# Two layers of a streaming encoder: a second buffer for a convolution's replicated input, the copies into it issued before the previous convolution, and one statistics pass for v

## The chip, the cores and the metric

The kernel runs on the 8 cores of one Trainium2 chip. Every core takes two prompt sequences of 2048 tokens and one sample group of 64 tokens; the cores do not talk to each other. The metric is the device time of the slowest core in microseconds (us), lower is better. Some executions, of the kernel before and of most of the others, were in a slower state: one die or both were granted a lower TensorE clock (in the slowest, of 5269 us, cores 0 to 3 had 0.806 to 0.808 and the others 0.972 to 0.974).

## The reference

Two layers, each with one projection of 13312 columns that feeds three branches, a gated merge and an output projection:

```python
h = rmsnorm(x, norm_g)
a_b, a_c, a_x, a_z, b_in, b_z, c_u, c_v, c_z, g_a, g_b, g_c = split(h @ w_in)
# A: short gated convolution of 3 taps
y_a = a_b * dwconv3(a_c * a_x) * silu(a_z)
# B: Conformer convolution module, 31 taps for each channel
glu = b_in[..., :W_B] * sigmoid(b_in[..., W_B:])
y_b = silu(layernorm(dwconv31(glu) + bias)) * silu(b_z)
# C: spatial gating over chunks of 128 tokens
v   = layernorm(gelu(c_v))
y_c = gelu(c_u) * (W_s @ v + b_s) * silu(c_z)
m = sum_k sigmoid(g_k + gate_b_k) * (y_k @ w_branch_k)
x = x + m @ w_out          # after two layers: a last rmsnorm
```

## The kernel before

A core cuts its tokens into nine tiles: five of 512 columns, three of 384 and, with the sample group, one of 448. I call one tile through one layer a *pass*; there are 18, in the order layer 0 of two tiles, layer 1 of the same two, then the next two tiles. Passes 1 to 9 and 11 have 512 columns, 10 and 12 to 16 have 384, the last two 448.

A helper records each operation with what it reads and writes, and derives the semaphores. So all ScalarE work has one line (L241), all TT work another (L244), and one reads by tile names. Four places matter.

**Branch B.** The 31-tap convolution is done by TensorE as 8 x 4 small matmuls with banded weights (`dB_t`, the taps). It needs the gated input four times, shifted by one column each (`grep`, made from `gluT` by 16 small copies that SyncE issues). A pair is two groups of 128 channels:

```python
grep = sb("grep", (128, 2, GB, PW), BF16)            # one buffer, one pair
def replicate(q):                                    # 16 copies, SyncE's queue
    for s4 in range(4):
        for g in range(GB):
            dma_start(out=grep[32*s4:32*s4+32, :, g, 0:wb],
                      in_=gluT[32*g:32*g+32, qb, :, s4:s4+wb])
def conv_b(j):                                       # reads grep and dB_t of j
    ...
    if j + 3 < 8: load_dB(j + 3)                     # taps, SyncE's queue, 3 buffers

stage_B1(0); replicate(0); stage_A(0)
for q in range(1, 4):
    stage_B1(q)
    conv_b(2*q-2); conv_b(2*q-1)
    replicate(q)                                     # after the convolutions that read grep
    stage_A(2*q-1); stage_A(2*q)
conv_b(6); conv_b(7); stage_A(7)
```

**v.** Gelu of a chunk of 128 tokens goes to `gv_t`, two buffers; after every second chunk `cv_stats` makes mean and 1/deviation (Sqrt on ScalarE, reciprocal on VectorE) and normalises two chunks.

**Weights.** They come as fp32 through GpSimd's queue (`wring<-w`, cast to bf16 on the way) until a block has been stored to memory as bf16 (`c<-wring`, SyncE's queue); from then on it is read as bf16 (`wring<-c`). Which visit of a block stores it is fixed by `(2, 0, 3, 1, 2, 1)[order % 6]`. A ring of four slots holds the blocks in use. A store is issued when its block is first used.

**Branch C and the merge.** co is normalised a stage at a time among branch C's stages; in the merge, m0+m1 is added after the third product.

## Time and profile before

| | before |
|---|---|
| median of 4 runs, one of them (4820.46) slow | 4750.1 us (4725.02 to 4820.46) |
| TensorE busy, profiled core | 4306.4 of 4726.6 us |
| granted clock, eight cores | 0.968 to 0.972 |

From the page of the kernel before: the span, TensorE's line of busy times, the digits of its busy share, of the granted clock and of the DMA engines in 40 slices, and the chain of work that ended last.

```profile
span 4726.6 us, 74121 instructions; the slowest of 8 cores (4691.4 to 4726.6 us)
PE 4306.4 (91%) x25860; PEld 2117.0 (45%) x25860; DVE 2024.8 (43%) x3476; ACT 1708.8 (36%) x2816; POOL 214.1 (5%) x607
PE   6897978979999999989999999989898999999897
PEclk8998999989999999999999999999999999999999
DMA  8898987988887658776574555474655555665453
PE 65%; DMA 10%; SPq 7%; DVE 7%; issue 6%; ACT 4%; DVEq 0%; POOL 0%; ACTq 0%; POOLq 0%
```

TensorE (PE) is the bottleneck, the DMA engines are nearly full in the first quarter only, and 17% of the chain is DMAs and their issuing.

The view of waits, TensorE alone, of the kernel before: who waited for whom, us in total, number of waits, longest.

```profile
PE ps L715 <- DMA grep<-gluT: 223.0, 32, 21.4
PE ps L507 <- ACT tmp_t L241: 46.5, 55, 2.6
PE ps L507 <- DVE tmp_t L247: 19.9, 43, 1.2
PE ps L897 <- DVE vm L244: 18.5, 18, 2.3
PE ps L557 <- DVE hT L244: 17.7, 6, 7.9
```

L715 is the convolution, L507 every projection, L897 the output projection. Over half of TensorE's 420 idle us is the convolution waiting for the copies.

One such wait in the timeline of TensorE, pass 6 of the kernel before (start, length, what, count, and in brackets the idle time before it and who ended it):

```profile
1534.75 16.57 PE L507 MATMUL ps<-hT,wring 128*128 128x512 bf16 x76
1561.73 6.07 PE L715 MATMUL ps<-grep,dB_t 128*32 128x512 bf16 x64 [10.41 <-DMA grep<-gluT]
```

TensorE stands still for 10.41 us, and then the 64 small matmuls take 6.07 us. Without a wait, 32 of them take 1.9 us. The record of the granted clock in the trace shows why: it stands at half from 1556.5 to 1566.7 us and at full afterwards.

The view of stretches of the kernel before, for passes 2 and 9 (512 columns) and 13 (384): window, its length, busy us of each engine with counts, granted clock, DMA share, GB/s.

```profile
336.00:627.00 291.00, 263.04 (x1430) 118.55 (x1428) 119.20 (x188) 100.26 (x172) 20.66 (x38) 0.96 0.91 188
2350.00:2615.00 265.00, 258.76 (x1422) 117.42 (x1420) 119.59 (x183) 98.18 (x150) 8.10 (x31) 1.00 0.54 175
3314.00:3533.00 219.00, 199.87 (x1379) 114.52 (x1378) 96.44 (x179) 84.33 (x146) 7.46 (x30) 0.98 0.61 203
```

Pass 9 shows what a 512-column pass costs when hardly anything waits: 258.76 us of work at clock 1.00. Pass 2 takes 26 us more, at 91% DMA.

### The profile page before, as it was taken

The numbers are of one execution on the slowest core, as the hardware profiler recorded it, in microseconds if no ns is written. First come the engines' busy times: TensorE is split into PE (matmuls) and PEld (weight loads), VectorE is DVE, ScalarE is ACT, GpSimd is POOL, SyncE is SP. The second block draws the span as 40 slices with busy tenths as digits, with TensorE's granted clock in tenths as the row PEclk, the third lists the DMA queues.
The fourth block names the chain that finished last, engine by engine and source line by source line (L and its number), as shares of the span: only waits on it lengthen the run. The fifth ranks groups of instructions, "written<-read, shape, count | busy, mean of one in ns | idle before, by whom it ended". The sixth has DMA issues, their size and how long they took to land.

```text
span 4726.6 us, 74121 instructions; the slowest of 8 cores (4691.4 to 4726.6 us)
## 1 busy us (share of the span) xinstructions
PE 4306.4 (91%) x25860; PEld 2117.0 (45%) x25860; DVE 2024.8 (43%) x3476; ACT 1708.8 (36%) x2816; POOL 214.1 (5%) x607
## 2 busy tenths in 40 slices
PE   6897978979999999989999999989898999999897
PEld 2343433434444444444444454445454555544444
DVE  2533534335353343535344353534344443545353
ACT  3332423334333342433343343334333433433332
POOL 1000000000000000000000000000000000000000
PEclk8998999989999999999999999999999999999999
DMA  8898987988887658776574555474655555665453
GB/s 174 159 175 194 186 166 156 176 208 187 206 204 193 190 167 197 176 203 198 169 221 143 193 184 181 146 225 171 217 184 191 192 189 193 212 200 178 150 175 127
DMA packets 234715, 869.22 MB, mean 184 GB/s; under 512 B 34512, under 2 KB 108848, under 8 KB 178032
## 3 DMA queue, kind: packets, MB, share of 16 engines
q1 hardware_dynamic: 195840, 648.75, 41.9%
q0 software_dynamic: 37952, 214.84, 25.0%
q8 instruction: 216, 3.54, 0.3%
q14 instruction: 147, 1.20, 0.1%
q10 hardware_dynamic: 560, 0.88, 0.1%
HBM read 874.87 MB, written 93.85 MB: 205 GB/s over the span
## 4 chain that ended last, share of the span: by engine, by line
PE 65%; DMA 10%; SPq 7%; DVE 7%; issue 6%; ACT 4%; DVEq 0%; POOL 0%; ACTq 0%; POOLq 0%
PE ps L507 50%; SPq L682 7%; PE ps L715 6%; DMA grep<-gluT 4%; PE ps L897 4%; PE ps L557 3%; DVE tmp_t L247 3%; DMA c<-wring 2%; DMA wring<-w 1%; ACT cs_t L241 1%; ACT L241 1%; ACT gv_t L241 1%; DVE co L244 1%; DVE yc L244 1%; PE ps L700 1%
## 5 line engine op out<-in xcount | busy, mean ns | idle before, releaser
L507 PE MATMUL ps<-hT,wring 128*128 128x512 bf16 (+2 forms) x13824 | 2770.7, 359 | 93.6 <-ACT tmp_t L241 46.5
L507 PEld LDWEIGHTS ps<-hT,wring 128*128 128x128 bf16 x13824 | 1343.3, 98 | 1438.0 <-issue 131.3
L241 ACT ACTIVATE tmp_t<-ps 128x512 f32<-128x512 f32 (+2 forms) x882 | 473.9, 556 | 938.6 <-PE ps L507 798.4
L247 DVE SCALAR_TENSOR_TENSOR tmp_t<-tmp_t,ps 128x512 f32<-128x512 f32 (+2 forms) x576 | 365.4, 634 | 827.3 <-PE ps L507 577.3
L241 ACT ACTIVATE tmp_t<-ps,pc 128x512 f32<-128x512 f32 (+2 forms) x432 | 274.9, 645 | 729.8 <-PE ps L507 729.5
L715 PE MATMUL ps<-grep,dB_t 128*32 128x512 bf16 (+2 forms) x5120 | 301.9, 390 | 239.0 <-DMA grep<-gluT 223.0
L244 DVE TENSOR_TENSOR tT<-ps,tmp_t 128x512 bf16<-128x512 f32 (+2 forms) x160 | 94.7, 592 | 843.5 <-PE ps L507 667.0
L241 ACT ACT_TABLE_LOAD x179 | 229.7, 1283 | 302.4 <-DVE tmp_t L247 95.6
L715 PEld LDWEIGHTS ps<-grep,dB_t 128*32 128x32 bf16 x5120 | 138.9, 107 | 399.0 <-issue 332.8
L241 ACT ACTIVATE co<-ps,pc 128x512 f32<-128x512 f32 (+2 forms) x144 | 93.1, 646 | 505.6 <-PE ps L715 505.4
L557 PE MATMUL ps<-wring,hT 128*128 128x512 bf16 (+1 forms) x1056 | 240.5, 389 | 23.0 <-DVE hT L244 17.7
L897 PE MATMUL ps<-wring,vm 128*128 128x512 bf16 (+1 forms) x1056 | 232.9, 381 | 20.6 <-DVE vm L244 18.5
L507 PE MATMUL ps<-yc,wring 128*128 128x512 bf16 (+2 forms) x1152 | 248.3, 358 | 0.0
L507 PE MATMUL ps<-yb,wring 128*128 128x512 bf16 (+2 forms) x1152 | 248.3, 358 | 0.0
L507 PE MATMUL ps<-ya,wring 128*128 128x512 bf16 (+2 forms) x1152 | 248.3, 358 | 0.0
L247 DVE SCALAR_TENSOR_TENSOR tmp_t<-tT,pc,tmp_t 128x512 f32<-128x512 bf16 (+2 forms) x320 | 208.5, 652 | 36.3 <-DVE tmp_t L247 1.6
L267 POOL DMA_DIRECT2D wring<-w x188 | 103.0, 548 | 1827.4 <-PE ps L507 1015.3
L557 PEld LDWEIGHTS ps<-wring,hT 128*128 128x128 bf16 (+1 forms) x1056 | 104.9, 100 | 153.3 <-issue 35.9
L241 ACT ACTIVATE cs_t<-ps,pc 128x512 bf16<-128x512 f32 (+2 forms) x288 | 169.4, 644 | 0.0
L897 PEld LDWEIGHTS ps<-wring,vm 128*128 128x128 bf16 (+1 forms) x1056 | 102.5, 98 | 145.8 <-issue 27.6
L241 ACT ACTIVATE xn_t<-X 128x1024 bf16<-128x1024 f32 (+1 forms) x99 | 103.7, 1050 | 176.0 <-DVE X L247 168.6
L507 PEld LDWEIGHTS ps<-yc,wring 128*128 128x128 bf16 x1152 | 112.7, 98 | 112.0
(101 smaller groups left out, 2525.2 us busy)
## 6 DMA issues: line engine op xcount, KB each, us to landing
wring<-c SPq DMA_DIRECT2D x284, 1024.0 KB, 6.2
wring<-c SPq DMA_DIRECT2D x212, 768.0 KB, 4.4
wring<-w POOLq DMA_DIRECT2D x112, 1024.0 KB, 11.7
wring<-w POOLq DMA_DIRECT2D x76, 768.0 KB, 9.4
c<-wring SPq DMA_DIRECT2D x44, 1024.0 KB, 10.6
grep<-gluT SPq DMA_DIRECT2D x640, 67.6 KB, 3.9
dB_t<-dball SPq DMA_DIRECT2D x128, 256.0 KB, 7.5
c<-wring SPq DMA_DIRECT2D x32, 768.0 KB, 9.1
```

The source lines that it names most:

```text
L241: S.op("act", lambda e: e.activation(out=out, in_=in_, func=func, **kw), reads=reads, writes=writes)
L244: S.op(eng, lambda e: e.tensor_tensor(out=out, in0=in0, in1=in1, op=op), reads=reads, writes=writes)
L247: S.op("dve", lambda e: e.scalar_tensor_tensor(out=out, in0=in0, scalar=scalar, in1=in1, op0=op0, op1=op1), reads=reads, writes=writes)
L267: S.op(eng, lambda e: e.dma_start(out=out, in_=in_), reads=reads, writes=writes, lane=lane)
L507: ins = e.matmul(bank_ap(b, NT), lhsT=w[:, kk, col0:col0 + 128], rhs=rhs[:, kk, 0:NT], start=(kk == 0), stop=(kk == 7))
L557: ins = e.matmul(ps[0:rows, (b2 + h) * 512:(b2 + h + 1) * 512], lhsT=hT[:, kk, c0:c0 + rows], rhs=wV[h][0][:, kk, :], start=(kk == 0), sto ...
L682: return e.dma_start(out=grep[32 * s4:32 * s4 + 32, :, g, 0:wb], in_=gluT[32 * g:32 * g + 32, qb, :, s4:s4 + wb])
L700: e.matmul(bank_ap(bS1, NT), lhsT=ones[:, :], rhs=cs_t[:, 2 * ci, 0:NT], start=(j == 0), stop=(j == 7))
L715: ins = e.matmul(ps[32 * g:32 * g + 32, b * 512 + c0:b * 512 + c0 + n], lhsT=dB_t[:, d, (g * MB + m) * 32:(g * MB + m + 1) * 32], rhs=grep ...
L897: ins = e.matmul(ps[0:rows, (b2 + h) * 512:(b2 + h + 1) * 512], lhsT=mT[:, kk, c0:c0 + rows], rhs=wO[h][0][:, kk, :], start=(kk == 0), sto ...
```

## The change

Its intent is to let the copies of a pair start before the previous convolution has ended and to put more work between them and the convolution. The space for the second buffer comes from `gv_t` and `cbq`. Several small edits come along. The diff, cut to its core:

```diff
-        grep = sb("grep", (128, 2, GB, PW), BF16)
+        grep = sb("grep", (128, 2, 2, GB, PW), BF16)
-        gv_t = sb("gv_t", (128, 2, D), F32)
-        cbq = sb("cbq", (128, DEPTH, NCH * GB * MB), F32)
+        cbq = fg[:, 0:DEPTH * NCH * GB * MB].rearrange("p (l n) -> p l n", l=DEPTH)
 # copies and convolution use grep[:, qb]; the order of the stages:
-  B1(0) rep(0) A(0) | B1(1) conv(0,1) rep(1) A(1) A(2) | B1(2) conv(2,3) rep(2) A(3) A(4)
-  | B1(3) conv(4,5) rep(3) A(5) A(6) | conv(6,7) A(7)
+  B1(0) rep(0) A(0) | B1(1) rep(1) A(1) conv(0,1) | B1(2) rep(2) A(2) conv(2,3)
+  | B1(3) rep(3) A(3) A(4) conv(4,5) A(5) conv(6,7) A(6) A(7)
 # v: gelu of chunk s goes to scratch tiles 2s, 2s+1; statistics once, after the last chunk
-            ACT(c(12), c(8), AF.Sqrt, ...); RECIP(c(16), c(12), ...)
+            ACT(c(12), c(8), AF.Ln, ...);   ACT(c(16), c(12), AF.Exp, ..., scale=-0.5)
-                if s % 2 == 1 or s == NS - 1:
-                    cv_stats(done, s + 1)
+            cv_stats()                       # after the loop; the same Ln, Exp in norm_rs
 # bf16 stores of weights, one block earlier (AHEAD = 1)
-            if n in to_store:
-                DMA(wloc(l, key, True)[0], wring[:, s, 0:8 * w], ...)
+            for i in range(n, n + AHEAD + 1):
+                if i in to_store: ...
 # branch C: co normalised every second stage, the last two in the z stages
-                if j < 6: co_norm(j + 2)
+                if j % 2 == 1: co_norm(2 + j // 2)
 # merge: m0 + m1 before the third product is there
+                    if i == 2: TT(m0, m0, m1, ALU.add, ...)
```

Left out: some preparations of the first two passes (a mask multiplication on VectorE in place of a GpSimd operation; two loads moved from GpSimd's queue to ScalarE's).

More of the change, by code (lines that the diff above doesn't have):

```diff
@@ L19 @@
 NTMP = 9
+AHEAD = 1
 GB = 4
@@ L227, in build_program @@
         ones = sb("ones", (128, 128), BF16)
+        tri = sb("tri", (128, 128), F32)
         epsc = sb("epsc", (128, 1), F32)
@@ L256, in TS @@
                                                     op1=op1), reads=reads, writes=writes)
-        def RECIP(out, in_, reads, writes):
-            S.op("dve", lambda e: e.reciprocal(out=out, in_=in_), reads=reads, writes=writes)
         def COPY(out, in_, reads, writes, eng="dve"):
@@ L321, in build_program @@
             plan += [(l, ("CV", 0)), (l, ("CV", 1))]
-            plan += [(l, ("B1", 0)), (l, ("A", 0))]
-            for q in range(1, 4):
-                plan += [(l, ("B1", q)), (l, ("A", 2 * q - 1)), (l, ("A", 2 * q))]
-            plan += [(l, ("A", 7))]
+            for q in range(4):
+                plan += [(l, ("B1", q)), (l, ("A", q))]
+            plan += [(l, ("A", j)) for j in range(4, 8)]
             plan += [(l, ("CUZ", q)) for q in range(4)]
@@ L375, in wget @@
             w = 384 if key[0] in B384 else 512
-            if n in to_store:
-                DMA(wloc(l, key, True)[0], wring[:, s, 0:8 * w], (("w", s),), (("wall", l, key),), "ws%d" % s)
+            for i in range(n, n + AHEAD + 1):
+                if i in to_store:
+                    to_store.discard(i)
+                    dst_bf, wi = wloc(plan[i][0], plan[i][1], True)
+                    si = i % NSLOT
+                    DMA(dst_bf, wring[:, si, 0:wi], (("w", si),), (("wall",) + plan[i],), "ws%d" % si)
             return wring[:, s, 0:8 * w].rearrange("p (k n) -> p k n", k=8), (("w", s),)
@@ L407, in build_program @@
         S.op("pool", lambda e: e.memset(ones[:], 1.0), writes=("ones",))
+        S.op("pool", lambda e: e.memset(tri[:], 1.0), writes=("tri",))
+        S.op("pool", lambda e: e.affine_select(out=tri[:], in_=tri[:], pattern=[[1, 128]], compare_op=ALU.is_ge, fill=0.0,
+                                               base=0, channel_multiplier=-1), reads=("tri",), writes=("tri",))
         S.op("pool", lambda e: e.memset(rid[:], 0.0), writes=("rid",))
@@ L415, in build_program @@
         ring_pump(2)
-        DMA(cbq[:, :, :], cvb_in.rearrange("l p n -> p l n"), (("X", 0, 1),), ("cbq",), "p1", eng="act")
+        DMA(cbq[:, :, :], cvb_in.rearrange("l p n -> p l n"), (("X", 0, 1),), ("fg",), "p1", eng="act")
         for l in range(DEPTH):
@@ L428, in prep_late @@
             DMA(chal_b[:, :, :, :].rearrange("p a b c -> p (a b c)"), cb_in, (), ("chal_b",), "p5", eng="pool")
-            DMA(fg[:, :], final_g.partition_broadcast(128), (), ("fg",), "p6", eng="act")
         def prep_loads(l):
-            DMA(ybf[:, 0:D], w_sq[l], (), ryb, "p2", eng="pool")
-            DMA(ycf[:, 0:D], b_s[l].partition_broadcast(128), (), ryc, "p2", eng="pool")
+            DMA(ybf[:, 0:D], w_sq[l], (), ryb, "p2", eng="act")
+            DMA(ycf[:, 0:D], b_s[l].partition_broadcast(128), (), ryc, "p3", eng="act")
         def prep_ws(l):
             wl = ybf[:, 0:D]
-            S.op("pool", lambda e: e.affine_select(
-                out=wl.rearrange("p (g q) -> p g q", g=8), in_=wl.rearrange("p (g q) -> p g q", g=8),
-                pattern=[[0, 8], [1, 128]], compare_op=ALU.is_ge, fill=0.0, base=0, channel_multiplier=-1),
-                reads=ryb, writes=ryb)
-            COPY(wsT[:, l].rearrange("p g q -> p (g q)"), wl, ryb, (("wsT", l),))
+            TT(wsT[:, l], wl.rearrange("p (g q) -> p g q", g=8), tri[:, :].unsqueeze(1).to_broadcast([128, 8, 128]), ALU.mult,
+               ryb + ("tri",), (("wsT", l),))
         def prep_bc(l):
@@ L464, in norm_rs @@
             r = lambda o: tuple(("st", c0 + o + s) for s in range(s0, s1))
-            ACT(st_s[:, c0 + 4 + s0:c0 + 4 + s1], st_s[:, c0 + s0:c0 + s1], AF.Sqrt, r(0) + ("epsc",), r(4), scale=1.0 / D,
+            ACT(st_s[:, c0 + 4 + s0:c0 + 4 + s1], st_s[:, c0 + s0:c0 + s1], AF.Ln, r(0) + ("epsc",), r(4), scale=1.0 / D,
                 bias=epsc[:, 0:1])
-            RECIP(st_s[:, c0 + 8 + s0:c0 + 8 + s1], st_s[:, c0 + 4 + s0:c0 + 4 + s1], r(4), r(8))
+            ACT(st_s[:, c0 + 8 + s0:c0 + 8 + s1], st_s[:, c0 + 4 + s0:c0 + 4 + s1], AF.Exp, r(4), r(8), scale=-0.5)
         def norm_xn(T, s):
@@ L523, in body, with gv, cv_stats @@
             wV = [wget(l, ("CV", 0)), wget(l, ("CV", 1))]
-            def cv_stats(s0, s1):
-                n = s1 - s0
-                r = lambda o: tuple(("st", 32 + o + s) for s in range(s0, s1))
-                c = lambda o: st_s[:, 32 + o + s0:32 + o + s1]
-                TS(st_s[:, 32 + s0:32 + s1], c(0), 1.0 / D, ALU.mult, r(0), r(0))
+            def gv(s, rows):
+                return tmp_t[0:rows, 2 * s:2 * s + 2, :].rearrange("p a n -> p (a n)"), RT(2 * s) + RT(2 * s + 1)
+            def cv_stats():
+                r = lambda o: tuple(("st", 32 + o + s) for s in range(NS))
+                c = lambda o: st_s[:, 32 + o:32 + o + NS]
+                TS(c(0), c(0), 1.0 / D, ALU.mult, r(0), r(0))
                 TS(c(4), c(4), 1.0 / D, ALU.mult, r(4), r(4))
@@ L532, in cv_stats @@
                 TT(c(8), c(4), c(8), ALU.subtract, r(4) + r(8), r(8))
-                ACT(c(12), c(8), AF.Sqrt, r(8) + ("epsc",), r(12), bias=epsc[:, 0:1])
-                RECIP(c(16), c(12), r(12), r(16))
+                ACT(c(12), c(8), AF.Ln, r(8) + ("epsc",), r(12), bias=epsc[:, 0:1])
+                ACT(c(16), c(12), AF.Exp, r(12), r(16), scale=-0.5)
                 STT(c(20), c(0), -1.0, c(16), ALU.mult, ALU.mult, r(0) + r(16), r(20))
-                for s in range(s0, s1):
-                    gi = s % 2
+                for s in range(NS):
                     rows = T["chunks"][s][1]
+                    gg, rg = gv(s, rows)
                     sc, bi_ = st_s[0:rows, 48 + s:49 + s], st_s[0:rows, 52 + s:53 + s]
-                    TS(v_t[0:rows, s, :], gv_t[0:rows, gi, :], sc, ALU.mult, (("gv", gi), ("st", 48 + s), ("st", 52 + s)),
-                       (("vm", s),), scalar2=bi_, op1=ALU.add)
+                    rs = rg + (("st", 48 + s), ("st", 52 + s))
+                    TS(v_t[0:rows, s, :], gg, sc, ALU.mult, rs, (("vm", s),), scalar2=bi_, op1=ALU.add)
                     if T["samp"] and s == NS - 1:
-                        gg = gv_t[0:rows, gi, :]
-                        TS(gg, gg, sc, ALU.mult, (("gv", gi), ("st", 48 + s), ("st", 52 + s)), (("gv", gi),), scalar2=bi_,
-                           op1=ALU.add)
-                        TT(gg, gg, ycf[0:rows, 0:D], ALU.mult, (("gv", gi),) + ryc, (("gv", gi),))
-                        TT(gg, gg, ycf[0:rows, D:2 * D], ALU.add, (("gv", gi),) + ryc, (("gv", gi),))
-                        DMA(nvs[l], gg, (("gv", gi),), (), "nv", eng="pool")
-            done = 0
+                        TS(gg, gg, sc, ALU.mult, rs, rg, scalar2=bi_, op1=ALU.add)
+                        TT(gg, gg, ycf[0:rows, 0:D], ALU.mult, rg + ryc, rg)
+                        TT(gg, gg, ycf[0:rows, D:2 * D], ALU.add, rg + ryc, rg)
+                        DMA(nvs[l], gg, rg, (), "nv", eng="pool")
             def cv_mm(s, h, b2):
@@ L574, in body @@
                 c0, rows = T["chunks"][s][0:2]
-                gi = s % 2
                 b2 = S.bank_n(2) if cvb is None else cvb[s]
@@ L578, in body @@
                     cv_mm(s, h, b2)
-                ACT(gv_t[0:rows, gi, :], ps[0:rows, b2 * 512:b2 * 512 + D], AF.Gelu_apprx_tanh, PSR(b2, b2 + 1),
-                    (("gv", gi), ("st", 32 + s)), accum_out=st_s[0:rows, 32 + s:33 + s])
-                ACT(cs_t[0:rows, 0:2, :].rearrange("p a n -> p (a n)"), gv_t[0:rows, gi, :], AF.Square, (("gv", gi),),
+                gg, rg = gv(s, rows)
+                ACT(gg, ps[0:rows, b2 * 512:b2 * 512 + D], AF.Gelu_apprx_tanh, PSR(b2, b2 + 1), rg + (("st", 32 + s),),
+                    accum_out=st_s[0:rows, 32 + s:33 + s])
+                ACT(cs_t[0:rows, 0:2, :].rearrange("p a n -> p (a n)"), gg, AF.Square, rg,
                     (("cs", 0), ("cs", 1), ("st", 36 + s)), accum_out=st_s[0:rows, 36 + s:37 + s])
-                if s % 2 == 1 or s == NS - 1:
-                    cv_stats(done, s + 1)
-                    done = s + 1
+            cv_stats()
+            S.tmp_ptr = 8
             wdone(l, ("CV", 0))
@@ L641, in load_dB @@
                         in1=rid[:, :].unsqueeze(1).to_broadcast([128, 32, 32]), op=ALU.mult),
-                        reads=("cbq", "rid"), writes=(("dB", d),))
+                        reads=("fg", "rid"), writes=(("dB", d),))
                     DMA(dball[l, j], dB_t[:, d, :], (("dB", d),), (("dball", l, j),), "dbs%d" % d)
@@ L681, in fn @@
                         def fn(e, s4=s4, g=g):
-                            return e.dma_start(out=grep[32 * s4:32 * s4 + 32, :, g, 0:wb],
+                            return e.dma_start(out=grep[32 * s4:32 * s4 + 32, qb, :, g, 0:wb],
                                                in_=gluT[32 * g:32 * g + 32, qb, :, s4:s4 + wb])
                         fns.append(fn)
-                S.dma_group("sp", fns, (("gluT", qb),), ("grep",), "rep%d" % qb)
+                S.dma_group("sp", fns, (("gluT", qb),), (("grep", qb),), "rep%d" % qb)
             bS1 = S.bank()
@@ L706, in conv_b @@
                 b = S.bank()
-                jj, d = j % 2, j % 3
+                qb, jj, d = (j // 2) % 2, j % 2, j % 3
                 def f(e):
@@ L716, in f @@
                                                lhsT=dB_t[:, d, (g * MB + m) * 32:(g * MB + m + 1) * 32],
-                                               rhs=grep[:, jj, g, d0 + 4 * m:d0 + 4 * m + n],
+                                               rhs=grep[:, qb, jj, g, d0 + 4 * m:d0 + 4 * m + n],
                                                start=(m == 0), stop=(m == MB - 1))
                     return ins
-                PE(f, ("grep", ("dB", d)), PSR(b))
+                PE(f, (("grep", qb), ("dB", d)), PSR(b))
                 ci = j % 2
@@ L744, in body, with hook, pair_B1, pair_conv @@
                 load_dB(j)
-            stage_B1(0)
-            replicate(0)
+            def hook():
+                if deferred:
+                    deferred.pop(0)()
+            def pair_B1(q):
+                stage_B1(q)
+                replicate(q)
+            def pair_conv(q):
+                conv_b(2 * q)
+                conv_b(2 * q + 1)
+            pair_B1(0)
             stage_A(0)
@@ L749, in body @@
                 prep_loads(bi)
-            for q in range(1, 4):
-                stage_B1(q)
-                if bi < DEPTH and q > 1:
-                    (prep_ws, prep_bc)[q - 2](bi)
-                if bi == 1 and q == 1:
-                    prep_late()
-                if bi == 1 and q == 3:
-                    cbh = chal_b[:, :, :, :].rearrange("p a b c -> p (a b c)")
-                    TS(cbh, cbh, 2.0, ALU.mult, ("chal_b",), ("chal_b",))
-                conv_b(2 * q - 2)
-                conv_b(2 * q - 1)
-                replicate(q)
-                for j in (2 * q - 1, 2 * q):
-                    stage_A(j)
-                    if deferred:
-                        deferred.pop(0)()
+            pair_B1(1)
+            stage_A(1)
+            if bi == 1:
+                prep_late()
+            hook()
+            pair_conv(0)
+            pair_B1(2)
+            if bi < DEPTH:
+                prep_ws(bi)
+            stage_A(2)
+            hook()
+            pair_conv(1)
+            pair_B1(3)
+            if bi == 1:
+                cbh = chal_b[:, :, :, :].rearrange("p a b c -> p (a b c)")
+                TS(cbh, cbh, 2.0, ALU.mult, ("chal_b",), ("chal_b",))
+            stage_A(3)
+            hook()
+            stage_A(4)
+            hook()
+            if bi < DEPTH:
+                prep_bc(bi)
+            pair_conv(2)
+            stage_A(5)
+            pair_conv(3)
             if bi == 0:
-                load_x(tiles[1], "pool", 1)
-            conv_b(6)
-            conv_b(7)
+                load_x(tiles[1])
+            if bi == 2:
+                DMA(fg[:, :], final_g.partition_broadcast(128), (), ("fg",), "p6", eng="pool")
             def stage_C(j, w, wres):
@@ L817, in co_norm @@
                 TT(c, c, rstd_bc[:, 0:NT], ALU.mult, (("co", j), "rstd_bc"), (("co", j),))
-            stage_A(7, stat_b)
+            stage_A(6, stat_b)
             ln_b()
+            stage_A(7)
             co_norm(0)
@@ L827, in body @@
                 stage_C(j, *wC)
-                if j < 6:
-                    co_norm(j + 2)
+                if j % 2 == 1:
+                    co_norm(2 + j // 2)
             def stage_Z(j, w, wres):
@@ L853, in body @@
                 stage_Z(j, *w)
+                if j % 2 == 0:
+                    co_norm(6 + j // 2)
             wdone(l, ("B2", 0))
@@ L870, in body @@
                 wR = wget(l, ("BR", j))
+                m0, m1, m2 = (tmp_t[:, t, 0:NT] for t in tsg)
                 for i, k in enumerate((0, 2, 1)):
@@ L873, in body @@
                     m = tmp_t[:, tsg[i], 0:NT]
+                    if i == 2:
+                        TT(m0, m0, m1, ALU.add, RT(tsg[0]) + RT(tsg[1]), RT(tsg[0]))
                     STT(m, m, 1.0, bank_ap(b, NT), ALU.add, ALU.mult, PSR(b) + RT(tsg[i]), RT(tsg[i]))
                 wdone(l, ("BR", j))
-                m0, m1, m2 = (tmp_t[:, t, 0:NT] for t in tsg)
-                TT(m0, m0, m1, ALU.add, RT(tsg[0]) + RT(tsg[1]), RT(tsg[0]))
                 TT(mT[:, j, 0:NT], m0, m2, ALU.add, RT(tsg[0]) + RT(tsg[2]), (("vm", j // 2),))
```

## The prediction

> **What bounds the kernel now.** TensorE: part 1 of the page has it busy 4306 of 4727 us, the others 43% or less. A change gains what it takes out of TensorE's 420 us of idle time, plus the slow clock after idle stretches (view of the cores: granted clock 0.97). The view of waits, TensorE alone: 223 us in 32 waits of branch B's convolution for its replicated input (grep<-gluT), the longest 21.4 us. The rest is small: 46.5 us for ScalarE's and 19.9 for VectorE's scratch work, 18.5 for vm before the output projection, 17.7 for hT, weights about 11.
>
> From the timeline, the waits before the first convolution pair sum to about 128 us, before the second to fourth 8, 33 and 44. SyncE needs about 10 us to issue the 16 copies (20 in early passes), they start only after the gating and land some 4 us later, while only two stages of 7 us (5.2 at 384 columns) lie between them and the first or last pair. The single buffer also keeps pairs 2 to 4 from being copied before the previous convolution ends.
>
> Second cost: [...] 32 convolution matmuls take 1.9 us, but 3.6 after a wait of over about 5 us. A 512-column pass (one tile through one layer) almost without waits has 258 us of TensorE work at clock 1.00; those with waits 261 to 266 at 0.94 to 0.98.
>
> **What changes.** Cover between copy and convolution grows from 14 to 21 us for pair 1, 21 to 25 for pair 2, 21 to 32 for pair 3, 14 to 25 for pair 4. Subtracting the extra cover leaves about 35 us of waits, nearly all before pair 1 of early passes: about 190 us go. Warm clock: some 25 stretches at 1.5 to 3 us, about 50 us. One statistics pass, fewer table loads (179 now at 1.28 us; I expect about 140), the earlier m0+m1 addition and later co normalisation act on engines with slack: 20 to 30 us of short TensorE waits. Copied, multiplied and loaded bytes stay.
>
> **What takes some back.** In the first five passes the DMA engines are 81 to 91% busy (view of stretches). The second holds 0.91 x 291 = 265 us of DMA work and can hardly go below 270; there I count little over half of the gain. SyncE's queue is in order: weight and tap loads will queue behind copies that follow each other sooner; at 384 columns pair 2's taps may come a microsecond late.
>
> **Sum.** First five passes -100 us, other 512-column passes -48, 384-column -80, last two -19: about -245 us, 5%. Predicted 4500 us, range 4415 to 4600; chances 0.90 faster, 0.09 same, 0.01 slower.
>
> **Signs that it is right.** The wait on grep<-gluT falls from 223 to under 60 us, what is left being pair 1 in early passes; granted clock about 0.985; TensorE busy 40 to 60 us less and 95 to 96% of the span; passes at 512 columns 260 to 265 us, at 384 203 to 206; DMA over 0.9 in the first five; table loads near 140; no new wait of the first branch-B stage on v's scratch.
>
> **What would make it wrong.** Early passes turning DMA-bound: waits for wring<-w of 50 us or more. Weight loads blocked behind copies. The statistics pass at the end of v's stage holding scratch that the first gating needs. A lower clock for the denser program: the passes with 258 us of work saw 1.00, so I doubt it.

The 50 us for the slow clock are the author's estimate, and the timeline of the kernel before has numbers for it: after a wait of 13.71 us in pass 2, 32 convolution matmuls took 3.60 us in place of 1.91, so 1.7 us more, and after the wait in pass 6 64 of them took 6.07 us in place of twice 1.91, so 2.3 us more.

## The result

| | before | after |
|---|---|---|
| median us | 4750.1 (4 runs) | 4510.02 (4 runs, 4508.02 to 4515.63) |
| ratio of fast runs | | 0.9513, 95% interval 0.9472 to 0.9554 |
| TensorE busy us, slowest core | 4306.4 | 4263.2 |
| granted clock, eight cores | 0.968 to 0.972 | 0.979 to 0.984 |
| TensorE idle us, median core | 362 | 200 |

The median of the kernel before includes its slow run; its three fast runs have a mean of 4742 us, those of the changed kernel 4511 us. A ratio here is the mean time of one kernel's fast runs over that of the other's fast runs of the same rounds, so not quite the ratio of the medians quoted. TensorE idle time is counted from the first matmul to the end of the last.

The time by stretch, from the starts of the passes in the traces, median of the eight cores, beside what the prediction had:

| us | before | after | difference | predicted |
|---|---|---|---|---|
| passes 1 to 5 | 1477.6 | 1418.6 | -59 | -100 |
| other five of 512 columns | 1363.6 | 1297.6 | -66 | -48 |
| six of 384 columns | 1301.6 | 1242.1 | -60 | -80 |
| last two | 524.2 | 497.0 | -27 | -19 |

The same lines of the page, for the changed kernel:

```profile
span 4510.4 us, 73823 instructions; the slowest of 8 cores (4484.6 to 4510.4 us)
PE 4263.2 (95%) x25860; PEld 2109.1 (47%) x25860; DVE 2009.6 (45%) x3317; ACT 1701.2 (38%) x2831; POOL 213.0 (5%) x604
PE   6998979979999999999999999999999999999898
PEclk8999989999999999999999999999999999999999
DMA  8899899998988759777574656475756566665463
PE 74%; DMA 10%; SPq 7%; DVE 3%; ACT 3%; issue 3%; DVEq 0%; POOL 0%; ACTq 0%; POOLq 0%
```

TensorE rises to 95% and its busy time falls by 43 us, because the clock is not lowered so often (39 stretches of TensorE work at half clock a core before, about 20 after, medians). But for two at the end, the digits that stay under 9 are in the first quarter, where the DMA digits stand at 8 and 9.

TensorE's waits in the changed kernel:

```profile
PE ps L713 <- DMA grep<-gluT: 84.7, 15, 22.2
PE ps L713 <- DMA dB_t<-dball: 48.0, 16, 11.2
PE ps L507 <- DVE tmp_t L248: 20.2, 15, 2.0
PE ps L556 <- DVE hT L245: 9.7, 6, 2.2
PE ps L920 <- DVE vm L245: 7.2, 8, 1.8
PE ps L507 <- ACT tmp_t L242: 1.2, 2, 0.6
```

Three things are to be seen. The wait for the copies fell from 223 to 84.7 us. A new one, for the taps (`dB_t<-dball`), took 48.0 us of that back. And the short waits of the projections for ScalarE's scratch work went from 46.5 to 1.2 us.

The stretches of passes 2, 9 and 13 in the changed kernel:

```profile
317.00:599.00 282.00, 262.64 (x1429) 118.58 (x1427) 119.27 (x181) 99.88 (x172) 18.98 (x34) 0.97 0.93 193
2234.00:2492.00 258.00, 256.94 (x1418) 116.69 (x1417) 118.57 (x173) 98.19 (x151) 8.03 (x31) 1.00 0.57 179
3166.00:3375.00 209.00, 198.46 (x1381) 114.81 (x1380) 95.42 (x171) 83.94 (x147) 7.45 (x30) 0.98 0.65 213
```

Pass 9 has reached TensorE's own time. Pass 2 is held at 282 us with the DMA engines 93% busy. Pass 13 still loses about 10 us, and TensorE's timeline there shows to what; the second view is SyncE's queue just before:

```profile
3235.23 5.36 PE L507 MATMUL ps<-hT,wring 128*128 128x384 bf16 x32
3244.27 2.75 PE L713 MATMUL ps<-grep,dB_t 128*32 128x384 bf16 x32 [3.68 <-DMA grep<-gluT]
3250.80 2.75 PE L713 MATMUL ps<-grep,dB_t 128*32 128x384 bf16 x32 [3.26 <-DMA dB_t<-dball]
```

```profile
3225.25 11.87 SPq L680 DMA_DIRECT2D grep<-gluT  x16
3237.26 0.98 SPq L265 DMA_DIRECT2D wring<-c  x2
3238.39 0.33 SPq L265 DMA_DIRECT2D dB_t<-dball  x1
```

The taps for the last convolution could be issued only at 3238.39 us, after 16 copies that took SyncE 11.87 us and two weight blocks. They landed 12.3 us after that, and the convolution that needed them began at once.

Where the remaining waits for the copies lie: before pair 1, in us, pass by pass (timeline of the slowest core).

| pass | 1 | 2 | 3 | 4 | 1 to 4 | 5 to 18 |
|---|---|---|---|---|---|---|
| before | 11.0 | 11.0 | 21.4 | 11.3 | 55 | 73 |
| after | 11.6 | 13.4 | 22.2 | 11.7 | 59 | 9 |

From pass 5 on the plan worked: 73 us became 9. In the first four passes the sum did not fall. That does not mean that the extra cover did nothing there. Over all eight cores the median of this sum is 50 us before and 57 after, but 72 us where branch B's part alone is undone and 74 us where only the old order is kept (both below): the other edits made these copies land later, and the new order took about as much back.

### The profile page after: what moved, and what is told of

Read it like the earlier page. It is cut to its first block, busy times and chain, and to the rows that moved or that the text cites. A ratio compares the mean times of both kernels' runs of the same rounds, so it can differ in the third digit from the quotient of the medians.

```text
span 4510.4 us, 73823 instructions; the slowest of 8 cores (4484.6 to 4510.4 us)
## 1 busy us (share of the span) xinstructions
PE 4263.2 (95%) x25860; PEld 2109.1 (47%) x25860; DVE 2009.6 (45%) x3317; ACT 1701.2 (38%) x2831; POOL 213.0 (5%) x604
## 3 DMA queue, kind: packets, MB, share of 16 engines
q1 hardware_dynamic: 195840, 648.75, 45.8%
## 4 chain that ended last, share of the span: by engine, by line
PE 74%; DMA 10%; SPq 7%; DVE 3%; ACT 3%; issue 3%; DVEq 0%; POOL 0%; ACTq 0%; POOLq 0%
PE ps L507 58%; SPq L680 7%; PE ps L920 5%; PE ps L556 5%; PE ps L713 4%; DMA dB_t<-dball 4%; DMA grep<-gluT 2%; DMA c<-wring 1%; DMA wring<-w 1%; DVE tmp_t L248 1%; ACT tmp_t L242 1%; ACT L242 1%; PE ps L698 1%; DMA X<-xp 1%; SPq L265 1%
## 5 line engine op out<-in xcount | busy, mean ns | idle before, releaser
L507 PE MATMUL ps<-hT,wring 128*128 128x512 bf16 (+2 forms) x13824 | 2770.5, 359 | 37.6 <-DVE tmp_t L248 20.2
L242 ACT ACTIVATE tmp_t<-ps 128x512 f32<-128x512 f32 (+3 forms) x948 | 548.0, 587 | 1077.0 <-PE ps L507 729.6
L713 PE MATMUL ps<-grep,dB_t 128*32 128x512 bf16 (+2 forms) x5120 | 274.4, 364 | 135.8 <-DMA grep<-gluT 84.7
L242 ACT ACT_TABLE_LOAD x161 | 206.6, 1283 | 211.1 <-DVE tmp_t L248 98.8
L248 DVE SCALAR_TENSOR_TENSOR gluT<-tmp_t,ps 128x512 bf16<-128x512 f32 (+2 forms) x160 | 93.8, 586 | 305.4 <-PE ps L507 252.1
## 6 DMA issues: line engine op xcount, KB each, us to landing
wring<-w POOLq DMA_DIRECT2D x112, 1024.0 KB, 11.6
```

The costliest lines, as they stand in the source:

```text
L242: S.op("act", lambda e: e.activation(out=out, in_=in_, func=func, **kw), reads=reads, writes=writes)
L248: S.op("dve", lambda e: e.scalar_tensor_tensor(out=out, in0=in0, scalar=scalar, in1=in1, op0=op0, op1=op1), reads=reads, writes=writes)
L507: ins = e.matmul(bank_ap(b, NT), lhsT=w[:, kk, col0:col0 + 128], rhs=rhs[:, kk, 0:NT], start=(kk == 0), stop=(kk == 7))
L713: ins = e.matmul(ps[32 * g:32 * g + 32, b * 512 + c0:b * 512 + c0 + n], lhsT=dB_t[:, d, (g * MB + m) * 32:(g * MB + m + 1) * 32], rhs=grep ...
```

## The experiments

Three questions: how much of the gain do the copies bring and how much the small edits; why do the first four passes keep their wait; can the new wait for the taps be taken away. Theory: the copies and the order bring most of it; the DMA engines, full with fp32 weights, hold the first copies back; the taps stand behind the copies in SyncE's queue. The rivals are named with each run. All eleven kernels gave correct results. The kernel before ran at 4728 to 4747 us in the fast runs. "Mean" is the mean of a kernel's fast runs; to be compared with 4511 us for the changed kernel, which was measured in other rounds. The intervals of the ratios are 0.2 to 0.4% to each side (0.9% for one, below), so a difference of two kernels in us is uncertain by some 20 us. Waits are those of the slowest core of the profiled run, unless said otherwise.

### Branch B's part undone

One buffer, copies after the previous pair, the old order of stages; all other edits kept.

```diff
-        grep = sb("grep", (128, 2, 2, GB, PW), BF16)
+        grep = sb("grep", (128, 1, 2, GB, PW), BF16)
-  B1(1) rep(1) A(1) conv(0,1) ...
+  B1(1) conv(0,1) rep(1) A(1) A(2) ...
```

> The changed kernel with branch B's part undone: one buffer for the replicated input, each copy after the previous convolution pair, the old order of the stages; all other edits kept. Theory (the copies and the order bring most of the gain): only the other edits remain, so about 70 us of the 240 us gained, 4650 to 4700 us, TensorE waiting about 220 us for grep<-gluT, other TensorE waits near 70 us as after the change. Rival (the statistics pass, the scratch and the small edits bring most): under 4590 us.

Three fast runs: 4641, 4610 and 4607 us, mean 4619, ratio 0.976 (interval 0.9665 to 0.9854, verdict unclear at 2%). Its waits:

```profile
PE ps L714 <- DMA grep<-gluT: 245.5, 35, 21.6
PE ps L508 <- ACT tmp_t L242: 7.4, 9, 0.9
```

Neither expectation held. By the means, the small edits alone brought 114 us (4733 to 4619) and not 70; branch B's part brought the other 108 us (4619 to 4511). The interval of this ratio is wide: the first number lies between 69 and 159 us, so it excludes the 20 to 30 us of the prediction, but not the 70 expected here. The short waits for ScalarE are mostly gone here too (46.5 us before), so they are not branch B's doing.

### Two buffers, old order

```diff
-  B1(1) rep(1) A(1) conv(0,1) | B1(2) rep(2) A(2) conv(2,3) | ...
+  B1(1) rep(1) conv(0,1) A(1) A(2) | B1(2) rep(2) conv(2,3) A(3) A(4) | ...
```

> The changed kernel with two buffers, each copy issued before the previous convolution pair, but the stages in the old order (two A stages between pairs, only one before the first pair). Theory (distance from copy to convolution matters): pairs 2 to 4 lose their waits, pair 1 keeps 110 to 130 us of waits on grep<-gluT, time 4560 to 4620 us. Rival (the second buffer alone does it): within 0.5% of the changed kernel, about 4510 us.

Three fast runs, mean 4567 us, ratio 0.9649 (0.9621 to 0.9677): in the range of the theory, half way. Its wait for the copies:

```profile
PE ps L714 <- DMA grep<-gluT: 187.2, 25, 22.8
```

By the timeline this is 133 us before pair 1 (expected 110 to 130), nothing before pairs 2 and 3, and 54 us before pair 4; with one buffer 137, 0, 34 and 74 us. So the second buffer took all of pair 3's wait, but pair 4, with two stages between its copies and it in the old order, kept most, against the theory. The buffer was worth about 53 us and the order about 56 us. In passes 1 to 4, pair 1 waited 77 us here and 59 us in the changed kernel, which has one stage of 7 us more as cover in each pass. The first five passes (median of the cores) took 1478 us before, 1494 with one buffer, 1448 here and 1419 after the change: as far as one profiled execution of each tells (that with one buffer was the slowest of its three fast runs), the small edits alone brought nothing there, and the gain of the first five passes came with branch B's part.

### Statistics of v after every two chunks

```diff
-            cv_stats()
+                if s % 2 == 1 or s == NS - 1:
+                    cv_stats(done, s + 1)     # two buffers in scratch tiles 0 to 3
```

> The changed kernel with v's statistics taken again after every two chunks, from two buffers in scratch space. Theory (the single pass frees the banks that the first branch-B stages need): TensorE's waits before the projections rise from about 38 us by 20 to 40 us, 16 to 36 more table loads, 4530 to 4560 us. Rival (that pass lies off TensorE's path): within 0.3% of 4510 us.

Four fast runs, mean 4562 us, ratio 0.9638 (0.9606 to 0.967), so about 50 us; table loads rose from 161 to 197. The wait that came back is the projections' for ScalarE (1.2 us in the changed kernel):

```profile
PE ps L507 <- ACT tmp_t L242: 24.6, 16, 3.9
```

The theory holds in kind; the loss was just over what was expected. By stretches it is 11 us in the first five passes, 7 in the other five of 512 columns, 21 in the six of 384, 9 in the last two, so about 2 us a pass at 512 columns and 3.5 at 384; why the narrower passes lose more was not looked into.

### Weight stores at their use

```diff
-AHEAD = 1
+AHEAD = 0
```

> The changed kernel with each bf16 weight store issued when its block is first used, not one block earlier. Theory (earlier stores free ring slots sooner for the fp32 loads of the first five passes, but TensorE hardly waits for weights): those passes 0 to 15 us longer in sum, within 0.4% of 4510 us, the wait of the GpSimd queue for c<-wring back from 124 us to over 250 us. Rival (the earlier stores are what made room in the early passes): over 4535 us, with TensorE waiting for wring<-w.

Of four runs, three fell in the slow state and one took 4576 us. Of the slow profile one thing is of use: in its sixth pass

```profile
1488.00:1800.00 312.00, 312.00 (x1424) 130.19 (x1423) 116.90 (x187) 96.16 (x148) 6.77 (x18) 0.81 0.57 155
```

the granted clock was 0.81 and no wait was left: TensorE was busy for all of the 312 us, and the waits that this study is about were gone there without any gain. The kernel was run again:

> The same kernel as a_store_at_use, of which only runs in the slow state and one of 4576 us were seen. Its first five passes took 1470 us, against 1426 us in the changed kernel, the TensorE clock not yet lowered. Expected now: 4545 to 4580 us in fast runs, the first five passes 35 to 55 us longer than in the changed kernel and the other thirteen within 10 us; if it is only the state of that chip, within 0.4% of 4510 us.

Four fast runs, mean 4587 us, ratio 0.9682 (0.965 to 0.9713, recorded verdict unclear): 76 us slower than the changed kernel, so the rival of the first expectation was right about the time. Its other half was not: TensorE did not wait for `wring<-w`. The loss is again the copies:

```profile
PE ps L713 <- DMA grep<-gluT: 127.9, 16, 21.6
```

The wait of GpSimd's queue for the stores (`c<-wring`) was 370.1 us, against 123.9 us in the changed kernel and 341.3 before. The first five passes took 48 us longer (1466.8 against 1418.6, median of the cores) and the other five of 512 columns 24 us; the second expectation had 35 to 55 us and, for all passes after the fifth, at most 10 us. The loss does not lie before pair 1: there the first four passes waited even less (42 us against 57, medians of the cores), but pairs 3 and 4 waited 15 and 45 us (0 and 10 in the changed kernel). A reading that fits: with late stores the fp32 loads start late, and more of them are then under way when the later copies are issued. That second step was not seen by itself.

### VectorE's order as before

```diff
-                if j % 2 == 1: co_norm(2 + j // 2)
+                if j < 6: co_norm(j + 2)
-                    if i == 2: TT(m0, m0, m1, ALU.add, ...)   # moved after the third product
```

> The changed kernel with two of its small edits on VectorE undone: co is normalised again one stage at a time during branch C (not one every second stage), and m0+m1 is added after the last product of the merge. Theory (in branch C, VectorE was what freed PSUM banks, so these edits removed short waits of TensorE): about 2 us of short waits per pass come back in branch C and half a microsecond before the output projection, together 30 to 45 us, 4540 to 4560 us. Rival (short waits there are hidden by the reserve of banks): within 0.3% of 4510 us.

Three fast runs, 4577, 4587 and 4603 us, mean 4589, ratio 0.9682 (0.9641 to 0.9724, recorded verdict unclear). That is 78 us over the changed kernel, but cores 4 and 5 of the profiled run spent pass 5 at a low clock (0.90 on core 5; 286 us with 2 to 3 us of waits; the others 270 to 274), and such passes may be in the timed runs too. The undisturbed cores are the better measure: by the median of the eight, 17, 18, 20 and 6 us more in the four stretches, together about 60 us. Core 1 (die 0) of this kernel:

```profile
PE ps L507 <- DVE tmp_t L248: 33.8, 48, 2.0
PE ps L507 <- ACT tmp_t L242: 26.5, 43, 0.9
PE ps L917 <- DVE vm L245: 17.9, 18, 2.3
```

In the changed kernel's core 1 these are 20.4 us for `tmp_t` of VectorE and 7.3 us for vm, and 1.2 us for ScalarE's. The theory holds in kind; it expected 30 to 45 us.

### Why pair 1 of the early passes still waits: all stores at the first visit

```diff
-            return (2, 0, 3, 1, 2, 1)[order.index(key) % 6]
+            return (0, 0, 0, 0, 0, 0)[order.index(key) % 6]
```

> The changed kernel, but every weight block is stored as bf16 at its first use, so that the second and fourth pass read no fp32 weights at all. Theory (what still delays the first copies in the first four passes is the backlog of fp32 loads in the DMA engines, not SyncE's issuing): the wait before pair 1, now 13.4 us in the second pass and 11.7 us in the fourth, falls under 3 us in both, while the first and third pass, with more stores, get 10 to 40 us longer; in sum 4490 to 4550 us. Rival (SyncE's 10 us of issuing is the cause): those two waits stay over 9 us.

One fast run, 4572.43 us, which was the profiled one; three were slow. The stretches of passes 1 to 4:

```profile
18.00:385.00 367.00, 281.78 (x1451) 122.60 (x1450) 130.87 (x189) 106.45 (x183) 22.96 (x43) 0.92 1.00 227
385.00:646.00 261.00, 257.94 (x1427) 117.17 (x1425) 119.00 (x180) 99.59 (x172) 1.59 (x3) 1.00 0.56 172
646.00:989.00 343.00, 275.70 (x1427) 119.85 (x1425) 124.70 (x178) 103.14 (x178) 19.23 (x36) 0.93 1.00 225
989.00:1247.00 258.00, 257.50 (x1426) 117.16 (x1425) 119.64 (x174) 107.03 (x184) 4.49 (x9) 1.00 0.57 181
```

In passes 2 and 4, without fp32 loads, pair 1 waits 0.0 us (13.4 and 11.7 in the changed kernel) though SyncE issues the same 16 copies; both passes run at TensorE's own time. The rival (SyncE's issuing) falls. Passes 1 and 3 hit 1.00 of the DMA engines, are 68 and 58 us longer than in the changed kernel, and TensorE waits 70.4 us for `wring<-w`; that was more than the 10 to 40 us expected, so the sum was over the expected range too.

How the engines share is visible in the DMA packets themselves. Counted from the trace of the changed kernel, pass 2, in windows of 3 us from the start of the pass: packets and MB that began in each, for GpSimd's queue (fp32 weights), SyncE's (the copies) and ScalarE's (two parameter loads).

| from us | GpSimd | SyncE | ScalarE |
|---|---|---|---|
| 31 | 41, 0.32 MB | 47, 0.03 MB | 26, 0.11 MB |
| 34 | 43, 0.35 MB | 43, 0.04 MB | 42, 0.17 MB |
| 37 | 54, 0.31 MB | 112, 0.09 MB | 111, 0.40 MB |
| 40 | 47, 0.39 MB | 47, 0.04 MB | 47, 0.18 MB |
| 43 | 38, 0.31 MB | 36, 0.03 MB | 36, 0.14 MB |
| 46 | 42, 0.24 MB | 217, 0.19 MB | 21, 0.05 MB |
| 49 | 3, 0.00 MB | 646, 0.62 MB | 5, 0.01 MB |

The packets here are the records of the profile, which took each row of a transfer, 8 KB for a weight load, as one. Where all three queues had work, they got nearly the same number of packets (43, 43 and 42 in the window from 34 us). In the window from 37 us GpSimd's queue had little work for a moment between two weight loads (from 38 to 39 us: 15, 59 and 57 packets), and the two others went faster at once. Here a packet of the weights carries about 8 KB and one of the copies about 1 KB, so the copies got about a ninth of the weights' bytes (0.04 MB beside 0.35 MB in the window from 34 us) until the backlog of the weights had run out, at about 48 us; then they went 15 times as fast (0.62 MB in the window from 49 us), and pair 1 started at 55.0 us.

### The fp32 loads in four pieces

```diff
-            DMA(wring[:, s, 0:w], src, (), (("w", s),), "w%d" % s, eng="pool")
+            h = w // 4      # four loads by columns: packets of 2 KB
+            S.dma_group("pool", [... wring[:, s, i*h:(i+1)*h] <- src[:, i*h:(i+1)*h] ...])
```

> The changed kernel with each fp32 weight load cut into four by columns, so that its DMA packets are 2 KB and not 8 KB long. Theory [...]: the waits before pair 1 in the first four passes fall from 59 to under 35 us; [...] 4470 to 4515 us. Rival (the engines are simply full, whoever is served first): those waits stay within 10 us of 59 us or grow, 4505 us or more.

An estimate: with as many packets of 2 KB for the weights as of about 1 KB for the copies, the copies would get half of the weights' bytes in place of a ninth.

The wait before pair 1 in passes 1 to 4 fell from 59 to 32.5 us, as the theory said, and in the same pass the copies now got 134 packets and 0.12 MB in the 3 us from 34 us, beside 136 packets and 0.25 MB of weights. But the time did not move: two fast runs, 4510.22 and 4501.89 us, ratio 0.9518 (0.9495 to 0.9541), and the first five passes took 1413.0 us against 1418.6. What the copies won, the weights lost (in the changed kernel `wring<-w` cost 3.2 us in all):

```profile
PE ps L715 <- DMA grep<-gluT: 43.4, 10, 13.2
PE ps L922 <- DMA wring<-w: 15.0, 3, 6.8
PE ps L509 <- DMA wring<-w: 8.9, 5, 6.3
```

So both were right in part: the theory about the waits, the rival about the time. In this run the size of the weights' packets changed who waited (32.5 us before pair 1 in place of 59, but 23.9 us for `wring<-w` in the two lines above in place of 3.2 in all), and not the time.

### Flat copies: half as many packets

```diff
-   out=grep[32*s4:32*s4+32, qb, :, g, 0:wb],              in_=gluT[32*g:32*g+32, qb, :, s4:s4+wb]
+   out=grep[32*s4:32*s4+32, qb, g] (flat)[:, 0:PW+wb],    in_=gluT[32*g:32*g+32, qb] (flat)[:, s4:s4+PW+wb]
```

> The changed kernel with the two channel groups of a pair lying one after the other in the replicated buffer, so that a copy moves one run of 2.1 KB a row in place of two of 1.1 KB: half the packets, 0 to 16% more bytes. Theory (the number of packets sets the time to landing): landing of a copy falls from 7.8 us to 4 to 5.5 us, the wait on grep<-gluT from 85 to under 50 us, on the taps from 48 to under 30 us, 4430 to 4475 us. Rival (bytes set it): landing and waits unchanged or worse, 4500 us or more.

Four fast runs, mean 4502 us, ratio 0.9508 (0.9473 to 0.9542): no difference from the changed kernel that the interval shows. SyncE's queue moved 158976 packets in place of 195840, but a copy at 512 columns landed after 8.3 us (7.8 in the changed kernel), and waits for copies and taps were 67.4 and 47.3 us (84.7 and 48.0). The rival, that bytes set the landing, is nearer.

### Taps on ScalarE's queue

```diff
-                    DMA(dB_t[:, d, :], dball[l, j], (("dball", l, j),), (("dB", d),), "db%d" % d)
+                    DMA(dB_t[:, d, :], dball[l, j], (("dball", l, j),), (("dB", d),), "db%d" % d, eng="act")
```

> The changed kernel with the loads of the convolution taps issued by ScalarE's queue right after the evacuation of the convolution, not by SyncE's behind the 16 copies. Theory (the taps come late because SyncE's queue serves them after the copies): TensorE's wait on dB_t<-dball falls from 48 us to under 10 us, no wait of that size replaces it, 4455 to 4485 us. Rival (the DMA engines are too busy with the copies for any queue to be quicker): the wait stays over 30 us, within 0.3% of 4510 us.

Two fast runs, 4485.38 and 4479.46 us, mean 4482, ratio 0.9468 (0.9445 to 0.9491); three slow. TensorE's longest waits now, and that for the taps:

```profile
PE ps L713 <- DMA grep<-gluT: 83.4, 20, 20.1
PE ps L507 <- DVE tmp_t L248: 20.6, 15, 2.0
PE ps L482 <- ACT xn_t L242: 16.9, 2, 13.5
PE ps L507 <- DVE tT L245: 14.3, 2, 8.4
PE ps L713 <- DMA dB_t<-dball: 5.7, 4, 2.7
```

The last line, from further down in the view, is the wait for the taps: 5.7 us (48.0 in the changed kernel). The six passes of 384 columns take 1205.5 us in place of 1242.1; the other stretches do not change by more than 6 us. The taps were late because of their place in SyncE's queue, not because of the load on the engines. Whether it was the later issue or the place behind the copies in the DMA engines, this run does not tell, since another queue changes both.

### Both, and both with later stores

> Taps on ScalarE's queue together with the flat copies of half as many packets. If their gains add (25 to 30 us from the taps, about 10 us from the flat copies): 4465 to 4480 us, the waits on grep<-gluT at 65 us or less. If the flat copies only relieved the queue that the taps stood in: 4480 us.

Four fast runs (4470, 4474, 4476 and 4497 us), mean 4479, ratio 0.9451 (0.9413 to 0.9488). With the median of the cores the first five passes take 1404.5 us and the 384-column ones 1208.7. With the next one it is the fastest kernel, 0.65% under the changed kernel by their ratios to the kernel before (0.9451 and 0.9513). The two were not run in the same rounds, and the intervals do not tell it from the kernel with the taps moved alone (0.9468); both expectations allow 4479, and the wait for the copies was 73.4 us, over the 65 of the first.

```diff
-            return (2, 0, 3, 1, 2, 1)[order.index(key) % 6]
+            return (3, 0, 3, 2, 2, 1)[order.index(key) % 6]
```

> The same with the stores of three of the six kinds of weight blocks moved a visit later or earlier, so that by the count of block transfers the second and fourth pass carry 8% less and the fifth to eighth more. Theory (the first four passes are bound by DMA bytes, the later have room): second and fourth pass 5 to 15 us shorter each, fifth to eighth up to 6 us longer each, in sum 4455 to 4475 us. Rival (the early passes are bound by the order in which the queue is served): no change against the kernel without it, or slower.

Two fast runs (4481 and 4476 us), mean 4479, ratio 0.9449, verdict unclear: nothing gained. Passes 2 and 4 became shorter (275 and 272 us, against 284 and 287 without it, slowest cores), as expected, but passes 5 to 8 gave it back: the other five passes of 512 columns took 1312.2 us against 1297.4. The later stores cost 26 more fp32 loads (214 in place of 188), so bytes were not only moved, but added.

## Why the prediction was right, point by point

The time (4500 predicted, 4510 measured) and the range were right. The sum was right in part by luck: errors of its terms cancel.

- **What bounds the kernel: right.** TensorE's idle time fell by 162 us (362 to 200, median of the cores), its busy time by 43 us (40 to 60 predicted), and that is the gain.
- **Slow clock after a wait: right in kind, its gain too large.** The granted clock rose from 0.97 to 0.98 (0.985 predicted). The trace of the kernel before shows both cases: the first pair of pass 6 took 6.07 us after its wait of 10.41 us, and that of pass 9, after a wait of 2.6 us, 3.6 us, no more than without a wait. Over the eight cores of the kernel before, 164 of TensorE's 165 waits of 5 us or more ended at half clock; of the 49 waits between 1.5 and 2 us two did, and between these lengths it varied. The stretches of TensorE work at half clock fell from 39 to about 20 a core, and half their length, an estimate of what they cost, from 78 to 45 us (medians): 34 us, where the prediction had about 50.
- **"Subtracting the extra cover leaves about 35 us of waits": wrong for the first four passes.** There, pair 1 waited 55 us before and 59 after. The step takes the landing time of the copies as fixed. In pass 2, with the DMA engines 93% busy, it was not: the copies got 0.03 to 0.09 MB in each 3 us from 31 to 46 us; they went faster when the backlog of fp32 weights had run out, at about 48 us, and pair 1 started at 55.0 us. Without that backlog the wait was 0.0 us. And the small edits moved the landing: in pass 2 the copies of pair 1 were issued from 24 or 25 to about 35 us after its start in all these kernels, but the convolution could start at 44 us before, at 54 with branch B's part undone and at 55 after (medians of the cores). With late stores it was 48 us, so the earlier stores are part of that; the rest was not tried apart. For passes 5 to 18 the step was right (73 to 9 us). My split of the waits by pair had also left out some 24 us before pair 3 in the first two passes; they went, as the waits before pair 3 did in all passes; and its 8 us before pair 2 were waits for VectorE (`tT`), not for the copies.
- **"At 384 columns pair 2's taps may come a microsecond late": right in kind, wrong in size.** The waits for the taps summed to 48.0 us, most of them before the second convolution of pair 4 and of pair 2. I had counted the issuing alone; in the case shown the tap load, issued behind 16 copies and two weight blocks, also landed late, 12.3 us after its issue. Taking the taps out of that queue gave 29 us back.
- **"20 to 30 us" for the statistics pass, VectorE's order and the rest: wrong, the largest error.** The small edits alone brought about 114 us (69 to 159 by the interval). Undone one at a time from the changed kernel, the single statistics pass is worth about 50 us, VectorE's order about 60, the earlier stores about 76. The sum is over 114, perhaps since they share waits with each other and with the copies, which no run shows. Ln and Exp in place of Sqrt and the reciprocal, and the preparations of the first two passes, were undone in no run. I had named the earlier stores nowhere in the sum, and credited the other two with engines' slack, though waits that they end (46.5 us for ScalarE's scratch work, 18.5 us for vm) stood in my own list.
- **About 190 us of waits for the copies go: too much.** They fell by 138 us, and 48 us of taps came in their place; branch B's part, as a whole, was worth about 108 us and not the 215 that the sum implies. This and the previous point cancel.
- **Early passes bound by DMA: right in kind, and more than allowed for.** The first five passes gained 59 us and not 100; their DMA shares were 0.91 to 0.95 in the first four and 0.87 in the fifth (over 0.9 predicted for all). The wait for the copies stayed at 84.7 us (under 60 predicted). And the sign that I named, waits for `wring<-w`, did not appear (3 us). The full engines show as waits for the copies, whose packets of about 1 KB got 0.04 MB beside 0.35 MB of weights in the window from 34 us of pass 2.
- **Table loads near 140: 161.** The single pass took 36 away (197 to 161). The new order of stages costs 18: both kernels with the old order have 143. What in the order causes it was not looked into; ScalarE is 38% busy.
- **No new wait of the first branch-B stage on v's scratch: right**; the waits for VectorE's `tmp_t` were 19.9 and 20.2 us.

What stays open: a schedule of stores between the two extremes that were tried. By share times length, passes 1 to 4 hold about 1079 us of DMA work in the changed kernel and 1003 us with all stores at the first visit, but there it is heaped on passes 1 and 3.

## What to carry to other kernels

Added distance can be subtracted from a wait for a transfer only where the transfer's landing time does not depend on what else is under way; where the DMA engines are full, ask what backlog is served beside it and in which packets, and look whether a wait that is removed comes back elsewhere: here, with smaller packets, the wait before pair 1 of the first four passes fell from 59 to 32.5 us and the time stayed (4506 us, mean of two runs, against 4511). When small transfers are moved together in one queue, look at what stands behind them: here the taps, for which another queue was the cure (48.0 us of waits before, 5.7 after). And short waits of the bottleneck engine, under a microsecond at a time, add up: the three kinds in the list before came to 85 us in 116 waits. Take them from the list at their full size before calling their cause slack.

## What else was measured

- The granted clock: in the changed kernel all eight cores had 0.979 to 0.984, with TensorE 95% busy (slowest core), and single passes had 1.00. A clock of 0.81 was seen, but only in some executions. Cores of one die could differ: in one fast run with VectorE's old order (4603 us) cores 4 and 5 had a mean of 0.969 and 0.968, and cores 6 and 7, of the same die, 0.981. And the clock changed within an execution: in the slow profile of the stores at their use core 7 stood at 0.97 in the fifth pass and at 0.81 in the sixth.
- The time that SyncE took to issue a DMA in the changed kernel: 0.59 us for a copy within the core's memory (median), up to 5.5 us, and about 0.32 us for a load of weights.
- A table load of ScalarE took 1283 ns, mean of 161.
